# Opening the SBUF pools of a two-layer decoder trunk in another order

## The chip, the cores and the metric

The kernel runs on one core of a Trainium2 chip. The metric is device microseconds of one execution, median of the runs shown. The engines are TensorE (PE, with PEld for its weight loads), VectorE (DVE), ScalarE (ACT), GpSimd (POOL) and SyncE (SP), which issues nearly all DMAs.

## What is computed

Two decoder layers on 256 positions of 1024 channels, in float32. Each layer adds three normed branches to x:

```
for l in range(2):
    x = x + 0.5 * rms_norm(swiglu(rms_norm(x, g), w_gate, w_up, w_down), post_g)    # FFN 1
    x = x + rms_norm(hybrid_mix(rms_norm(x, g), w_in, ..., w_out), post_g)          # mixer
    x = x + 0.5 * rms_norm(swiglu(rms_norm(x, g), w_gate, w_up, w_down), post_g)    # FFN 2

def swiglu(h, w_gate, w_up, w_down):        # 1024 -> 2816 -> 1024
    return (silu(h @ w_gate) * (h @ w_up)) @ w_down
```

`hybrid_mix` projects the normed x to 2688 columns, runs four head groups over them (a gated convolution, a gated spatial mixing, an RWKV-7 recurrence in chunked form, a 31-tap convolution module), concatenates their 1024 channels and multiplies by `w_out`.

## The kernel before, in words

**Products.** Every large product is made from three float32r matmuls. A weight tile `raw` (128 x 1024 float32) is loaded by a DMA that SP issues, ACT rounds it to `whi`, DVE writes the rest `raw - whi` to `wlo` (`split`, lines 129 to 145). The left operand is split the same way into a high and a low part. `mm3` (lines 147 to 150) then adds three matmuls into one PSUM bank:

```
nc.tensor.matmul(dst, lhsT=sh, rhs=hi[:, c0:c0 + n], start=start, stop=False)   # L148
nc.tensor.matmul(dst, lhsT=sh, rhs=lo[:, c0:c0 + n], start=False, stop=False)   # L149
nc.tensor.matmul(dst, lhsT=sl, rhs=hi[:, c0:c0 + n], start=False, stop=stop)    # L150
```

`lhsT` is the stationary operand (128 x 128, loaded by a weight load of its own), `rhs` the moving one (mostly 128 x 512, that is 2048 contiguous bytes of each partition). Four kinds of product use it, and the profile names them by their PSUM tile:

- `pgu`: gate and up projection of an FFN. Stationary `xh`/`xl` (the normed x, pool `act`), moving `whi`/`wlo` (pool `wp`). 24 matmuls go to one bank before the next.
- `dn`: down projection of an FFN. Stationary `hh`/`hl` (made in `TR`, pool `work`, tag `c2`), moving `whi`/`wlo`. Each three matmuls change the bank, between two of the banks of tag `acc`.
- `pin`: input projections of the mixer. Stationary `xh`/`xl`, moving `whi`/`wlo`, 512, 384 or 256 columns.
- `wo`: output projection of the mixer. Stationary `yh`/`yl` (pool `wp`, tag `w2`), moving `whi`/`wlo`; like `dn` it changes between two banks each three matmuls, for block 1 in banks of the same tag `acc`.

Smaller float32 matmuls (transposes, the recurrence) fill the mixer's middle.

**Order of the work.** An FFN works on 11 slices of 256 hidden columns; for slice i it runs `pgu` for the position blocks 0 and 1 with the transposes of slice i-1 between them, and then `dn` of slice i-1 for both blocks. DMAs are issued by SP in program order, each when its `raw` buffer (4 of them) is free. The order of instructions on each engine is set by the framework's scheduler and by the places where the program pins an order.

**Pools.** A pool is a stretch of each SBUF partition. The pools lie one after another in the order in which they are opened (lines 52 to 56), and a tile takes the next multiple of 32 bytes:

```
const = ctx.enter_context(tc.tile_pool(name="const", bufs=1))
wp = ctx.enter_context(tc.tile_pool(name="wp", bufs=14))
rawp = ctx.enter_context(tc.tile_pool(name="rawp", bufs=4))
act = ctx.enter_context(tc.tile_pool(name="act", bufs=1))
work = ctx.enter_context(tc.tile_pool(name="work", bufs=2))
```

`const` ends at byte 20160 of the partition, in both kernels. The others hold, per partition:

| pool | what | bytes | bytes over a multiple of 64 |
|---|---|---|---|
| `wp` | 24 tiles of 4096 (`whi`, `wlo`, `yh`, `yl`, PB, PK, ...) | 98304 | 0 |
| `rawp` | 4 tiles `raw` of 4096 | 16384 | 0 |
| `act` | x, `xh`, `xl`, gp, ..., pc, zT, caT, zc | 54688 | 32 (caT takes 2080 bytes; of these tiles only zc lies behind it) |
| `work` | tags f2, f1, c2 (`hh`, `hl`), c1 and small ones | 37184 | 0 |

Within its pool every tile keeps its place. So the byte where a tile starts follows from where its pool starts. The tags f2, f1 and c2 of `work` start multiples of 64 bytes behind the pool's start.

Of the kernel before, what the change touches and what calls it, by code (L numbers as in the profile page):

```python
# [48 lines left out]
def trunk_kernel(ctx: ExitStack, tc: tile.TileContext, a, out):  # L49
    nc = tc.nc  # L50

    const = ctx.enter_context(tc.tile_pool(name="const", bufs=1))
    wp = ctx.enter_context(tc.tile_pool(name="wp", bufs=14))
    rawp = ctx.enter_context(tc.tile_pool(name="rawp", bufs=4))
    act = ctx.enter_context(tc.tile_pool(name="act", bufs=1))
    work = ctx.enter_context(tc.tile_pool(name="work", bufs=2))
    ps = ctx.enter_context(tc.tile_pool(name="ps", bufs=2, space=bass.MemoryType.PSUM))

    def acc_bank(name):
# [1069 lines left out]
```

## Time and profile before

| | us |
|---|---|
| median of 3 runs | 1041.27 (1040.5 to 1042.33) |
| the profiled execution | 1041.07 |
| its span, first to last instruction | 1039.3 |
| PE busy | 1015.2 (98%) |
| DVE, ACT, POOL busy | 668.1, 533.3, 69.5 |

The profile is of one execution. A matmul's end in it is modelled, so its duration (some 392 ns) overlaps the next one; what matmuls cost is read from their starts. The 1.8 us between the profiled execution's time and its span lie ahead of and behind the instructions.

### The profile page before, as it was taken

The page shows a single profiled execution, that of the slowest core. Times are in us where ns is not written, and L with a number is a line of the kernel's source. Part 1 is how long each engine was busy: PE and PEld are TensorE (multiplying, and loading weights), DVE is VectorE, ACT ScalarE, POOL GpSimd, SP SyncE. Part 2 cuts the span into 40 slices and gives each one's busy share as a digit, 9 for nine tenths or more (in the row PEclk, how much of TensorE's full clock was granted, in tenths as well). Part 3 has the DMA queues.
Part 4 walks back from the last instruction along what each step waited for, and adds up shares of the span by engine and source line. Part 5 has one row for each costly group of instructions (what it writes and reads, how often), then busy time and mean ns, then how long its engine had stood idle before and what let it go on. Part 6 is the DMA issues. An engine that isn't in the chain of part 4 may idle for free.

```text
span 1039.3 us, 13405 instructions
## 1 busy us (share of the span) xinstructions
PE 1015.2 (98%) x4898; PEld 832.2 (80%) x4898; DVE 668.1 (64%) x1044; ACT 533.3 (51%) x824; POOL 69.5 (7%) x133
## 2 busy tenths in 40 slices
PE   8999999999999999999999999999999999999997
PEld 6788888788797788888787888887878887888885
DVE  5765453689988755545575555447999885545533
ACT  7655353567466644535464435336655665444421
POOL 1000000210022100000010000013000130000000
PEclk9999999999999999999999999999999999999999
DMA  7985655344045756565556565635522367556521
GB/s 277 303 289 166 210 166 186 106 152 160 24 145 180 243 172 213 162 207 169 170 195 205 167 208 164 210 111 167 167 85 81 122 199 227 202 164 209 165 71 40
DMA packets 51474, 178.28 MB, mean 172 GB/s; under 512 B 6097, under 2 KB 6609, under 8 KB 51409
## 3 DMA queue, kind: packets, MB, share of 16 engines
q1 hardware_dynamic: 51120, 176.91, 52.2%
q8 instruction: 38, 0.62, 0.2%
q10 hardware_dynamic: 288, 0.52, 0.1%
q14 instruction: 28, 0.22, 0.1%
HBM read 176.36 MB, written 1.05 MB: 171 GB/s over the span
## 4 chain that ended last, share of the span: by engine, by line
PE 83%; DVE 8%; DMA 4%; ACT 2%; POOL 1%; issue 1%; SPq 0%; DVEq 0%; POOLq 0%; ACTq 0%
PE pgu L149 13%; PE pgu L150 13%; PE pgu L148 13%; PE dn L149 8%; PE dn L148 8%; PE dn L150 8%; DMA raw<-in_ffn 4%; PE pin L149 3%; PE pin L148 3%; PE pin L150 3%; PE hTp L348 2%; DVE wlo L141 1%; PE zp L676 1%; PE wo L148 1%; PE xT L178 1%
## 5 line engine op out<-in xcount | busy, mean ns | idle before, releaser
L141 DVE TENSOR_TENSOR wlo<-raw,whi 128x1024 fp32r<-128x1024 f32 (+1 forms) x320 | 388.8, 1219 | 161.8 <-ACT whi L140 146.3
L140 ACT CAST whi<-raw 128x1024 fp32r<-128x1024 f32 (+1 forms) x320 | 334.1, 1047 | 204.2 <-PE dn L149 107.6
L148 PE MATMUL pgu<-whi,xh 128*128 128x512 f32 x704 | 279.2, 397 | 2.7 <-ACT xh L237 2.2
L149 PE MATMUL pgu<-wlo,xh 128*128 128x512 f32 x704 | 275.6, 392 | 1.4 <-DVE wlo L141 1.4
L150 PE MATMUL pgu<-whi,xl 128*128 128x512 f32 x704 | 275.2, 391 | 0.0
L148 PEld LDWEIGHTS pgu<-whi,xh 128*128 128x128 f32 x704 | 132.6, 188 | 30.9 <-ACT xh L237 2.4
L149 PEld LDWEIGHTS pgu<-wlo,xh 128*128 128x128 f32 x704 | 132.5, 188 | 28.8 <-DVE wlo L141 2.1
L150 PEld LDWEIGHTS pgu<-whi,xl 128*128 128x128 f32 x704 | 132.4, 188 | 28.5
L148 PE MATMUL dn<-whi,hh 128*128 128x512 f32 x352 | 140.1, 398 | 3.8 <-ACT hh L352 3.8
L337 DVE SCALAR_TENSOR_TENSOR h<-pgu,rpre,silu 128x256 f32<-128x256 f32 x88 | 42.4, 482 | 153.1 <-ACT silu L335 152.9
L149 PE MATMUL dn<-wlo,hh 128*128 128x512 f32 x352 | 140.1, 398 | 0.0
L335 ACT ACTIVATE silu<-pgu,rpre 128x256 f32<-128x256 f32 x88 | 41.6, 472 | 188.7 <-PE pgu L150 187.4
L150 PE MATMUL dn<-whi,hl 128*128 128x512 f32 x352 | 136.8, 392 | 0.0
L148 PEld LDWEIGHTS dn<-whi,hh 128*128 128x128 f32 x352 | 66.2, 188 | 21.0 <-ACT hh L352 5.1
L150 PEld LDWEIGHTS dn<-whi,hl 128*128 128x128 f32 x352 | 65.8, 188 | 16.6 <-DVE hl L353 1.2
L149 PEld LDWEIGHTS dn<-wlo,hh 128*128 128x128 f32 x352 | 66.1, 188 | 14.7
L149 PE MATMUL pin<-wlo,xh 128*128 128x512 f32 (+2 forms) x192 | 70.8, 371 | 0.0
L148 PE MATMUL pin<-whi,xh 128*128 128x512 f32 (+2 forms) x192 | 70.5, 371 | 0.0
L150 PE MATMUL pin<-whi,xl 128*128 128x512 f32 (+2 forms) x192 | 70.5, 371 | 0.0
L835 DVE SCALAR_TENSOR_TENSOR zc<-zT,par,zc 128x256 f32<-128x256 f32 x120 | 49.8, 477 | 3.2 <-ACT zc L832 3.2
L149 PEld LDWEIGHTS pin<-wlo,xh 128*128 128x128 f32 x192 | 36.0, 188 | 5.4 <-DVE wlo L141 0.7
L150 PEld LDWEIGHTS pin<-whi,xl 128*128 128x128 f32 x192 | 36.3, 189 | 5.1 <-DVE xl L190 0.6
(216 smaller groups left out, 892.2 us busy)
## 6 DMA issues: line engine op xcount, KB each, us to landing
raw<-in_ffn SPq DMA_DIRECT2D x260, 512.0 KB, 4.5
raw<-in_wout SPq DMA_DIRECT2D x16, 512.0 KB, 4.4
raw<-in_win_z SPq DMA_DIRECT2D x8, 512.0 KB, 4.1
raw<-in_win_rk SPq DMA_DIRECT2D x8, 512.0 KB, 4.6
raw<-in_win_ca SPq DMA_DIRECT2D x8, 512.0 KB, 4.1
raw<-in_win_uv SPq DMA_DIRECT2D x8, 512.0 KB, 4.4
gp<-in_post_g SPq DMA_DIRECT2D x6, 512.0 KB, 4.8
raw<-in_win_vl SPq DMA_DIRECT2D x8, 384.0 KB, 3.2
```

The costliest lines, as they stand in the source:

```text
L140: i0 = nc.scalar.copy(hi[:, 0:n], raw[:, 0:n])
L141: i1 = nc.vector.tensor_tensor(out=lo[:, 0:n], in0=raw[:, 0:n], in1=hi.bitcast(F32)[:, 0:n], op=ALU.subtract)
L148: nc.tensor.matmul(dst, lhsT=sh, rhs=hi[:, c0:c0 + n], start=start, stop=False)
L149: nc.tensor.matmul(dst, lhsT=sh, rhs=lo[:, c0:c0 + n], start=False, stop=False)
L150: nc.tensor.matmul(dst, lhsT=sl, rhs=hi[:, c0:c0 + n], start=False, stop=stop)
L178: t = nc.tensor.transpose(tp[:, k * P:(k + 1) * P], x[b][:, kk * P:(kk + 1) * P], ident)
L335: nc.scalar.activation(out=s, in_=pg[:, 0:256], func=AF.Silu, scale=r)
L337: nc.vector.scalar_tensor_tensor(out=h, in0=pg[:, 256:512], scalar=r, in1=s, op0=ALU.mult, op1=ALU.mult)
L348: nc.tensor.transpose(tp[:, q * P:(q + 1) * P], h[:, j * P:(j + 1) * P], ident)
L676: nc.tensor.matmul(zp[:, h * P:(h + 1) * P], lhsT=PB[b][:, h, 1, :], rhs=S["Xm"][:, h, :], start=True, stop=True)
L835: nc.vector.scalar_tensor_tensor(out=zc[:, j, :], in0=zT[:, j, k:k + 256], scalar=w, in1=zc[:, j, :], op0=ALU.mult, op1=ALU.add)
```

## The change

After `const` the pools are opened in the order `work`, `act`, `wp`, `rawp`. Nothing else in the program is edited.

```
     const = ctx.enter_context(tc.tile_pool(name="const", bufs=1))
+    work = ctx.enter_context(tc.tile_pool(name="work", bufs=2))
+    act = ctx.enter_context(tc.tile_pool(name="act", bufs=1))
     wp = ctx.enter_context(tc.tile_pool(name="wp", bufs=14))
     rawp = ctx.enter_context(tc.tile_pool(name="rawp", bufs=4))
-    act = ctx.enter_context(tc.tile_pool(name="act", bufs=1))
-    work = ctx.enter_context(tc.tile_pool(name="work", bufs=2))
```

By the sizes above the pools start at these bytes:

| pool | before | over a multiple of 64 | after | over a multiple of 64 |
|---|---|---|---|---|
| `wp` | 20160 | 0 | 112032 | 32 |
| `rawp` | 118464 | 0 | 210336 | 32 |
| `act` | 134848 | 0 | 57344 | 0 |
| `work` | 189536 | 32 | 20160 | 0 |

## Rows read from the trace of the kernel before

**Rows 1.** The page: busy time, and the chain that ended last.
```profile
PE 1015.2 (98%) x4898; PEld 832.2 (80%) x4898; DVE 668.1 (64%) x1044; ACT 533.3 (51%) x824; POOL 69.5 (7%) x133
PE 83%; DVE 8%; DMA 4%; ACT 2%; POOL 1%; issue 1%; SPq 0%; DVEq 0%; POOLq 0%; ACTq 0%
```

**Rows 2.** Stages: time from:to, then busy us of PE, PEld, DVE, ACT, POOL; clock; DMA.
```profile
36.00:190.00 154.00, 154.00 (x690) 125.61 (x689) 86.51 (x88) 72.90 (x85) 3.11 (x4) 1.00 0.62 203
200.00:330.00 130.00, 125.66 (x741) 105.49 (x740) 117.77 (x283) 80.83 (x160) 17.21 (x35) 1.00 0.41 131
```

**Rows 3.** Groups by line and shape, one of each kind of three-matmul product.
```profile
L148 PE MATMUL pgu<-whi,xh 128*128 128x512 f32 x704 | 279.2, 397 | 2.7 <-ACT xh L237 2.2 <-ACT whi L140 0.4 <-ACT whi L279 0.2
L149 PE MATMUL dn<-wlo,hh 128*128 128x512 f32 x352 | 140.1, 398 | 0.0
L148 PE MATMUL pin<-whi,xh 128*128 128x512 f32 x128 | 51.0, 398 | 0.0
L149 PE MATMUL wo<-wlo,yh 128*128 128x512 f32 x64 | 26.1, 408 | 0.0
L148 PE MATMUL pin<-whi,xh 128*128 128x384 f32 x32 | 11.0, 344 | 0.0
L148 PE MATMUL pin<-whi,xh 128*128 128x256 f32 x32 | 9.2, 287 | 0.0
```

**Rows 4.** Timeline of PE, start first: pgu alone, ends of a run of 70.
```profile
337.98 0.39 PE L150 MATMUL pgu<-whi,xl 128*128 128x512 f32 x1
...
353.62 0.39 PE L150 MATMUL pgu<-whi,xl 128*128 128x512 f32 x1
```

**Rows 5.** Timeline of PE: a run of 24 dn and the pgu behind it.
```profile
101.97 0.39 PE L148 MATMUL dn<-whi,hh 128*128 128x512 f32 x1
102.20 0.40 PE L149 MATMUL dn<-wlo,hh 128*128 128x512 f32 x1
102.44 0.39 PE L150 MATMUL dn<-whi,hl 128*128 128x512 f32 x1
102.67 0.39 PE L148 MATMUL dn<-whi,hh 128*128 128x512 f32 x1
...
107.57 0.40 PE L148 MATMUL pgu<-whi,xh 128*128 128x512 f32 x1
```

**Rows 6.** Timeline of PE: wo of block 0, ends of a run of 14.
```profile
323.06 0.39 PE L148 MATMUL wo<-whi,yh 128*128 128x512 f32 x1
...
326.01 0.39 PE L149 MATMUL wo<-wlo,yh 128*128 128x512 f32 x1
```

**Rows 7.** Groups by line and shape: equal DVE and ACT operations on differently placed operands.
```profile
L190 DVE TENSOR_TENSOR xl<-xg,xh 128x512 fp32r<-128x512 f32 x20 | 13.2, 689 | 0.5 <-ACT xh L189 0.4
L189 ACT CAST xh<-xg 128x512 fp32r<-128x512 f32 x20 | 11.9, 617 | 5.5 <-DVE xg L182 5.4
L281 DVE TENSOR_TENSOR wlo<-raw,whi 128x512 fp32r<-128x512 f32 x8 | 5.3, 689 | 5.7 <-ACT whi L279 5.7
L279 ACT CAST whi<-raw 128x512 fp32r<-128x512 f32 x8 | 4.7, 616 | 3.9 <-DMA raw<-in_ffn 3.9
```

**Rows 8.** DMA issues: KB each, median us from issue to landing.
```profile
raw<-in_ffn SPq DMA_DIRECT2D x8, 256.0 KB, 5.4
xt<-in_xT SPq DMA_DIRECT2D x4, 256.0 KB, 5.5
```

**Rows 9.** The chain in order of time, mixer of layer 0: float32 matmuls of 128 columns.
```profile
280.04 1.79 PE zp L676 x16
...
284.32 0.89 PE wps L691 x8
```

**Rows 10.** Waits of PE itself: us in total, times, longest.
```profile
PE dn L148 <- ACT hh L352: 3.8, 3, 1.9
...
PE pgu L149 <- DVE wlo L141: 1.4, 2, 0.8
...
PE pgu L148 <- ACT whi L140: 0.4, 1, 0.4
```

## The prediction, made before the changed kernel was run

> **What bounds the kernel now.** The page first: PE is busy for 98% of the span and holds 83% of the chain that ended last, while DVE and ACT are busy for two thirds and half [rows 1]. [...] So the time is the sum of the distances from one matmul's start to the next. No instruction, wait or DMA is edited; the change can act only through what an operand's place in the partition does to the speed of an instruction. The question is which instructions care.
>
> The groups give the counts: three lines each of 704 `pgu`, 352 `dn`, 192 `pin` (128 + 32 + 32) and 64 `wo` [rows 3], that is 2112, 1056, 576 and 192 matmuls. Their listed means overlap (ends are modelled), so I read starts. An undisturbed run of `pgu` goes from 337.98 to 353.62 us in 69 steps, 226.7 ns each [rows 4]. A run of `dn` goes from 101.97 to 107.57 in 24 steps, 233.3 ns each, and evenly so: each three take 0.70 us [rows 5]. That is 6.7 ns more for the same 512 columns from the same weight pool. `wo` takes 226.9 (2.95 us in 13 steps) [rows 6]. `wo` is built as `dn` is (three matmuls to a bank, then the other bank) and reads the same moving tiles; block 1 of it writes the same kind of banks. What sets `dn` apart from both is where its stationary operand lies: `hh` and `hl` start 32 bytes over a multiple of 64, `xh`, `xl`, `yh`, `yl` and all moving tiles on one. I take that as the cause, short of proof: no other float32r matmul here has an operand off 64.
>
> **The change part by part.** There is one edit with these consequences: weights and raw tiles go from 64-byte starts to 32 over, the work pool from 32 over onto 64, the activations stay on 64 (only zc stays off it).
>
> *DVE and ACT: nothing.* The 128x512 subtraction takes 689 ns with `xg` (work pool, 32 over) and 689 with all operands on 64; the 128x512 cast takes 617 against 616 [rows 7]. If a nanosecond were there, it would lie behind PE.
>
> *DMA: nothing.* 256 KB loads into `xt` (32 over) land after 5.5 us, into `raw` (on 64) after 5.4, in the same stretch of the start [rows 8]. The difference is within their queueing; were it 0.1 us a load, the buffers ahead would cover it except at the FFN starts.
>
> *float32 matmuls: nothing.* `zp` reads both operands on 64: 1.79 us for 16 records, 112 ns. `wps` has its moving operand `zz` 32 over: 0.89 us for 8, 111 ns [rows 9].
>
> *float32r matmuls.* The stationary part has a price: 6.7 ns. The part that matters most, a moving operand 32 over, has no row: all 3936 read theirs on 64 before. [...] A gain from it I exclude by nothing but find no reason for. I take 6.7 ns: it is the nearest row, of the same instruction form and the same offset, and a stream of 2048 bytes meets the same boundaries as a load of 512. Then:
>
> - `pgu`: 2112 x 6.67 ns = +14.1 us (stationary on 64 as before, moving now off).
> - `pin`: 576 x 6.67 = +3.8 (the step taken as the same for 256 and 384 columns).
> - `dn`: the stationary comes onto 64 (-7.0), the moving goes off it (+7.0): 0.
> - `wo`: both operands go off. Two prices would be +2.6; if what counts is that the two differ, 0. I take one, +1.3.
>
> Sum +19.2 us. From it goes what is hidden: at the start of three FFNs and at the first slices of the kernel PE waits for weights that come by DMA, 3.8 + 1.4 + 0.4 us in all [rows 10]. The 70 `pgu` ahead of such a wait grow by 0.47 us each time, and the wait shrinks by that: some -1.4 over three. Elsewhere nothing hides a longer matmul, since PE is the chain. Net +17.8 on the profiled execution's 1041.07, which is 0.2 below the median of the runs: **1059**. The likeliest case's own range: without `wo` and with all 5.6 us of waits shrinking 14.1 + 3.8 - 5.6 = +12.3, with `wo` at 2.6 and nothing hidden +20.5: 1053 to 1062.
>
> **The rivals.**
>
> *Only the stationary operand's place counts (faster).* The price of `dn` is paid during the weight load's overlap with the stream, and the stream itself would run at its rate wherever it starts. Then `dn` gains 1056 x 6.67 = 7.0 us and `wo`, whose `yh`/`yl` move with `wp`, loses 1.3: -5.7, and another -1.5 or so if the uneven first steps of `pgu` behind each `dn` run go too; 1034 to 1036. For it: the float32 rows, where a moving operand off 64 is free [rows 9]. It decides where the moving price is under 5.7 / 3936 = 1.5 ns. The same sign comes if not the 64 bytes but the high end of the partition is what slows `hh`/`hl`, for `work` moves to the low end; then the last of the weight slots would pay instead.
>
> *The place counts for nothing (no change).* Then `dn` has its 233.3 ns for another reason, such as a state of PE's queues that its waits set up, and the time stays at 1041. For it: DVE, ACT, DMA and float32 matmuls all ignore the offset [rows 7 to 9]. Against it: `wo` with the same structure settles at 226.9 [rows 6]. [...] That the schedule itself could change with the addresses, so that more than addresses differ, I count here with a small part: the scheduler works with buffers of tags, which are the same.
>
> *The moving operand costs more than 6.7 ns*, say twice: +38 us, 1079. Nothing in the trace asks for it.
>
> **How the numbers follow.** Forecast (both operands count, or their difference does) 0.47; stationary alone or high end 0.30; no effect 0.19; twice the price 0.04. About 0.2% (2.1 us) is what a measurement of this kernel can tell from no change. Slower gets 0.47 + 0.04 = 0.51, less a little for a moving price so small that `dn`'s gain cancels it: 0.50. Faster 0.30. Same 0.20. Cases of both signs hold most of the chance, so the range reaches from the stationary-only case to the upper end of the forecast: 1034 to 1063, beside 1053 to 1062 for the likeliest alone.
>
> **What would show it.** If the forecast is right, runs of `pgu` show steps of 233 ns instead of 226.7 and `dn` stays at 233; PE stays at 98%; DVE, ACT and DMA rows keep their durations. If the stationary alone counts, `pgu` stays at 226.7 and `dn` comes down to 227. `wo` tells one price (233) from two (240) or none (227). If `dn` keeps 233 and `pgu` 227, the place isn't the cause. I am wrong in the mechanism if DVE or ACT durations move, or if the order of instructions differs.

## The result, and the profile after

The changed kernel takes **1053.48 us** (median of 4 runs, 1052.45 to 1054.64), beside 1041.8 for the kernel before on the same chip (4 runs, 1040.5 to 1044.8): a ratio of **1.0108 [1.0083, 1.0134]**, slower by 11.7 us. The profiled execution took 1052.45 us, with a span of 1050.7, 11.4 more than before. One run among all those below, of the last experiment, took 1725.28 us at a granted clock of 0.616, and its median and ratio leave it out.

The page of the changed kernel, busy time and the chain that ended last, to read against [rows 1]:

```profile
PE 1028.6 (98%) x4898; PEld 835.0 (79%) x4898; DVE 667.7 (64%) x1044; ACT 533.0 (51%) x824; POOL 69.5 (7%) x133
PE 85%; DVE 7%; DMA 3%; ACT 2%; POOL 1%; issue 1%; SPq 0%; DVEq 0%; POOLq 0%; ACTq 0%
```

Same counts, and each engine has its instructions in the same order as before. PE alone is busier, by 13.4 us. DVE, ACT and POOL are not. The granted clock of the two stages of [rows 2] is 1.00 again. The groups by line and shape, the same four as in [rows 7]:

```profile
L190 DVE TENSOR_TENSOR xl<-xg,xh 128x512 fp32r<-128x512 f32 x20 | 13.1, 686 | 0.5 <-ACT xh L189 0.4
L189 ACT CAST xh<-xg 128x512 fp32r<-128x512 f32 x20 | 11.9, 616 | 5.6 <-DVE xg L182 5.5
L281 DVE TENSOR_TENSOR wlo<-raw,whi 128x512 fp32r<-128x512 f32 x8 | 5.3, 688 | 5.7 <-ACT whi L279 5.7
L279 ACT CAST whi<-raw 128x512 fp32r<-128x512 f32 x8 | 4.6, 612 | 3.9 <-DMA raw<-in_ffn 3.9
```

Here the placings have swapped (`xg` is on 64 now, `raw`, `whi` and `wlo` are 32 over) and the durations stay within 4 ns: 686 and 688 ns on DVE, 616 and 612 on ACT. The DMA issues of the start, as [rows 8] (KB each, median us to landing), and PE's longest wait for ACT, as the first of [rows 10]:

```profile
raw<-in_ffn SPq DMA_DIRECT2D x8, 256.0 KB, 5.6
xt<-in_xT SPq DMA_DIRECT2D x4, 256.0 KB, 5.1
```

```profile
PE dn L148 <- ACT hh L352: 2.8, 3, 1.1
```

`raw` went from 5.4 to 5.6 and `xt` from 5.5 to 5.1. In the runs below the medians go from 5.0 to 5.8 for `raw` and from 4.8 to 6.1 for `xt`, with no order by place, so no effect of the place shows. The wait at the FFN starts fell from 3.8 to 2.8 us. So the time lies in the distances between matmul starts. The timeline of PE, start first: a run of 24 `dn` with the `pgu` behind it, 14 `wo`, and a run of 70 `pgu`, as [rows 4 to 6]:

```profile
103.33 0.39 PE L148 MATMUL dn<-whi,hh 128*128 128x512 f32 x1
...
108.92 0.40 PE L148 MATMUL pgu<-whi,xh 128*128 128x512 f32 x1
...
326.02 0.39 PE L148 MATMUL wo<-whi,yh 128*128 128x512 f32 x1
...
328.96 0.39 PE L149 MATMUL wo<-wlo,yh 128*128 128x512 f32 x1
...
341.07 0.40 PE L150 MATMUL pgu<-whi,xl 128*128 128x512 f32 x1
...
357.24 0.40 PE L150 MATMUL pgu<-whi,xl 128*128 128x512 f32 x1
```

`pgu` takes 16.17 us for 69 steps, 234.3 ns each instead of 226.7. `dn` stays at 233 (5.59 us in 24). `wo` stays at 226 (2.94 us in 13), though now both its operands lie 32 over a multiple of 64. The table sums all start-to-start distances of the two profiled executions, each counted for the matmul that begins it. The last column is what the distances above 260 ns (waits and hand-overs) hold beyond a step of 227 ns each, a step being the distance from one start to the next:

| product | before, us | after, us | difference | of it, shorter stalls |
|---|---|---|---|---|
| `pgu`, 2112 | 494.2 | 506.0 | +11.8 | -0.6 |
| `pin`, 576 | 127.1 | 127.7 | +0.6 | -0.6 |
| `dn`, 1056 | 247.3 | 247.2 | -0.1 | 0.0 |
| `wo`, 192 | 50.9 | 50.9 | 0.0 | -0.1 |
| all other matmuls | | | -1.0 | |
| sum | | | +11.4 | |

Practically all of it is `pgu`. The question left is why `pgu` pays, `dn` stays and `wo` does not pay. Below, the settled step of a run of matmuls is the mean step once its pattern repeats.

### The profile page after: what moved, and what is told of

Read it like the earlier page. It is cut to its first block, busy times and chain, and to the rows that moved or that the text cites. A ratio compares the mean times of both kernels' runs of the same rounds, so it can differ in the third digit from the quotient of the medians.

```text
span 1050.7 us, 13405 instructions
## 1 busy us (share of the span) xinstructions
PE 1028.6 (98%) x4898; PEld 835.0 (79%) x4898; DVE 667.7 (64%) x1044; ACT 533.0 (51%) x824; POOL 69.5 (7%) x133
## 4 chain that ended last, share of the span: by engine, by line
PE 85%; DVE 7%; DMA 3%; ACT 2%; POOL 1%; issue 1%; SPq 0%; DVEq 0%; POOLq 0%; ACTq 0%
PE pgu L149 14%; PE pgu L148 14%; PE pgu L150 14%; PE dn L148 8%; PE dn L150 8%; PE dn L149 8%; PE pin L149 3%; DMA raw<-in_ffn 3%; PE pin L148 3%; PE pin L150 3%; PE hTp L348 2%; PE zp L676 1%; PE wo L148 1%; PE wo L149 1%; PE xT L178 1%
## 5 line engine op out<-in xcount | busy, mean ns | idle before, releaser
L148 PE MATMUL pgu<-whi,xh 128*128 128x512 f32 x704 | 283.5, 403 | 1.9 <-ACT xh L237 1.5
L149 PE MATMUL pgu<-wlo,xh 128*128 128x512 f32 x704 | 280.3, 398 | 1.6 <-DVE wlo L141 1.4
L150 PE MATMUL pgu<-whi,xl 128*128 128x512 f32 x704 | 279.3, 397 | 0.0
L148 PEld LDWEIGHTS pin<-whi,xh 128*128 128x128 f32 x192 | 36.3, 189 | 5.4 <-ACT whi L140 0.4
```

## The experiments

All of them pad tiles by some bytes, which moves what lies behind; no instruction changes its form or its place in its engine's order. Ratios are against the kernel before, run on the same chip. Where a sum of distances is given it is of the profiled execution.

### Does each operand's own place modulo 64 count?

**Work pool onto 64, everything else as before.** The pool order of before, zc padded by 32 bytes at the end of `act`:

```
-        zc = act.tile([P, 2, 256], F32, name="zc")
+        zc = act.tile([P, 520], F32, name="zc")[:, 0:512].rearrange("p (j t) -> p j t", j=2)
```

> Pools in the order of before, with 32 bytes more at the end of act, so that hh/hl come onto a multiple of 64 and every operand of the three-matmul products lies on one; hh/hl stay at the high end of the partition. Difference theory (a step is 226.7 ns once settled where both operands start at the same place within 64 bytes, 233 to 234 otherwise): dn falls from 233.4 to about 227, 1056 x 6.4 = -6.8 us, and the uneven first steps of pgu behind each dn settle sooner, -1.5: ratio to before 0.992. Theory that each operand off 64 costs on its own: the same. Theory that only the moving operand counts and dn has a reason of its own: dn stays at 233, ratio 1.000. Theory that the high end of the partition slows hh/hl: also 1.000.

Measured: 1036.97 us, ratio 0.9953 [0.9935, 0.9971]. Faster, but by less than expected: `dn` lost 4.0 us, not 6.8. Its run in the timeline, 24 steps:

```profile
102.06 0.39 PE L148 MATMUL dn<-whi,hh 128*128 128x512 f32 x1
...
107.56 0.39 PE L148 MATMUL pgu<-whi,xh 128*128 128x512 f32 x1
```

5.50 us in 24 steps is 229 ns, in an even pattern of 229, 232, 226. With every operand of `dn` on 64 the step should have been 227. So 64 bytes is not the whole of it: there are more than two levels. The high end of the partition isn't the reason either, since `hh` and `hl` still lie there.

**Everything 32 bytes over.** A constant padded, so that every pool behind it moves; distances between tiles stay:

```
-    dpar = const.tile([P, L, 8], F32, name="dpar")
+    dpar = const.tile([P, L, 12], F32, name="dpar")
```

> Pools in the order of before, with 32 bytes more in const: all other pools move by 32. Weights, raw, activations lie 32 over a multiple of 64, hh/hl on one. Difference theory: pgu, pin and wo have both operands off alike and stay at 227, dn still differs and stays at 233: ratio 1.000 (within 0.002). Each operand off 64 costs: pgu has two prices, at least +11.8 us as the moving one alone gave in the changed kernel, ratio 1.012 or more. Only the moving one counts: 1.011.

Measured: 1042.38 us, ratio 1.0002 [0.9989, 1.0016]. The timeline, a run of 24 `dn` and 69 steps of `pgu`:

```profile
103.83 0.39 PE L148 MATMUL dn<-whi,hh 128*128 128x512 f32 x1
...
109.43 0.40 PE L148 MATMUL pgu<-whi,xh 128*128 128x512 f32 x1
...
339.93 0.39 PE L150 MATMUL pgu<-whi,xl 128*128 128x512 f32 x1
...
355.58 0.39 PE L150 MATMUL pgu<-whi,xl 128*128 128x512 f32 x1
```

`pgu` at 15.65 / 69 = 226.8 ns with both operands 32 over a multiple of 64, and `dn` at 5.60 / 24 = 233.3 with the stationary now on 64 and the moving operand over. Nothing changed where only absolute places did. So the reading that each operand pays for its own place modulo 64 fails.

### Is it the difference of the two places?

**Moving operand alone over.** The same constant and the x of block 0 padded by 32 bytes each, so that `xh` and `xl` come back onto a multiple of 64; `wp` is moved by 32 bytes, `hh` by 64 and so stays 32 over:

```
-    x = [act.tile([P, D], F32, name=f"x{b}") for b in range(NB)]
+    x = [act.tile([P, D + 8 * (b == 0)], F32, name=f"x{b}")[:, 0:D] for b in range(NB)]
-    dpar = const.tile([P, L, 8], F32, name="dpar")
+    dpar = const.tile([P, L, 12], F32, name="dpar")
```

> Pools in the order of before, with 32 bytes more in const and 32 more ahead of x1: weights and raw 32 over a multiple of 64, xh/xl on one, hh/hl 32 over as before. So pgu and pin differ, dn and wo have both operands off alike. Difference theory: pgu 234 (+11.8 us), pin +0.6, dn 227 (-6.8), wo unchanged: +5.6 us, ratio 1.005. Only the moving one counts: pgu +11.8, dn at 233 or more: 1.011. Each operand off 64 costs: dn pays twice, about 240, +11.8 + 7: 1.018.

Measured: 1047.5 us, ratio 1.0045 [1.0031, 1.0059]. The same stretches:

```profile
102.24 0.40 PE L148 MATMUL dn<-whi,hh 128*128 128x512 f32 x1
...
107.75 0.40 PE L148 MATMUL pgu<-whi,xh 128*128 128x512 f32 x1
...
339.21 0.40 PE L150 MATMUL pgu<-whi,xl 128*128 128x512 f32 x1
...
355.31 0.39 PE L150 MATMUL pgu<-whi,xl 128*128 128x512 f32 x1
```

`pgu` rises to 16.10 / 69 = 233.3 ns (+9.1 us in all), `dn` falls to 5.51 / 24 = 229.6 (-3.7 us). The ratio is the 1.005 expected by the difference modulo 64, but its parts are not: +11.8 and -6.8 were expected, and `dn` at 227.

**New pool order, both operands on 64.** The changed kernel with the 32-byte pad of zc, which puts `wp` on a multiple of 64 again:

> Pools in the order of the change, with 32 bytes more at the end of act: wp and rawp come onto a multiple of 64, so every operand of the three-matmul products lies on one. Difference theory, and the theory that each operand off 64 costs: pgu 227, dn 227: ratio to before 0.992, the same as the old order with all on 64; the order of the pools is then worth nothing by itself. If the order or the far end of the partition costs something of its own, it stays above 1.000. If the granule is 128 or 256 bytes (xh/xl and whi/wlo start 64 apart here), pgu stays at 234.

Measured: 1046.75 us, ratio 1.0039 [1.0022, 1.0055]: a miss for the difference modulo 64, which expected 0.992. Of what was expected, only the last alternative, a granule of 128 or 256 bytes, has `pgu` stay dear.

```profile
102.72 0.40 PE L148 MATMUL dn<-whi,hh 128*128 128x512 f32 x1
...
108.19 0.40 PE L148 MATMUL pgu<-whi,xh 128*128 128x512 f32 x1
...
339.63 0.39 PE L150 MATMUL pgu<-whi,xl 128*128 128x512 f32 x1
...
355.74 0.39 PE L150 MATMUL pgu<-whi,xl 128*128 128x512 f32 x1
```

`pgu` stays at 16.11 / 69 = 233.5 ns (+10.6 us) with both operands on 64, and `dn`, also with both on 64, settles at 227 after seven uneven steps (-5.0 us). If it is the difference of the two starts that counts, its period must be longer than 64 bytes: here `pgu` has a distance of 64 bytes modulo 256, and `dn` of 0.

Ordered by that distance (start of the stationary tile less start of the moving one, modulo 256), the runs so far agree with each other. Distances 0, 32, 160 and 192 each occur at two pairs of places, and each has one step to within 0.3 ns, so it is the distance that counts and not the places:

| kernel, product | stationary, moving, modulo 256 | distance | settled step, ns |
|---|---|---|---|
| before, `pgu` | 192, 192 | 0 | 226.7 |
| everything 32 over, `pgu` | 224, 224 | 0 | 226.8 |
| new order on 64, `dn` | 192, 192 | 0 | 226.7 |
| after, `dn` | 192, 160 | 32 | 233 |
| moving alone over, `pgu` | 0, 224 | 32 | 233.3 |
| new order on 64, `pgu` | 0, 192 | 64 | 233.5 |
| after, `pgu` | 0, 160 | 96 | 234.3 |
| before, `dn` | 96, 192 | 160 | 233.3 |
| everything 32 over, `dn` | 128, 224 | 160 | 233.3 |
| work pool on 64, `dn` | 128, 192 | 192 | 229 |
| moving alone over, `dn` | 160, 224 | 192 | 229 |

### How long is the period?

**Work pool 256 bytes apart, and 0 apart, modulo 512.** The pool order of before, zc with 96 bytes of padding (first kernel) and with 352 (second); the edit is that of the first experiment with 536 and 600 for 520:

> Pools in the order of before, 96 bytes more at the end of act: hh/hl start 256 bytes apart from whi/wlo when both starts are taken modulo 512 (modulo 256 they agree). The runs so far say that the step depends on the distance of the two starts, and on more of it than the last 64 bytes. If the period is 256 bytes: dn settles at 226.7 ns as wo does, 1056 x 6.7 = -7.0 us, and pgu behind it settles sooner, -1.5: ratio 0.992. If it is 512 bytes or more: dn stays between 229 and 234, ratio 0.995 to 1.000.

> Pools in the order of before, 352 bytes more at the end of act: hh/hl start at the same place as whi/wlo and xh/xl modulo 512, so all products but the short float32 ones have distance 0. Distance theory, whatever its period up to 512: dn settles at 226.7 ns, ratio 0.992, about 1033 us. If dn had a reason of its own beside the distance, it stays above 229 as with 192 bytes distance: 0.995.

Measured: 1034.52 us, ratio 0.9930 [0.9910, 0.9951], and 1034.7 us, ratio 0.9928 [0.9909, 0.9947]. They agree within their intervals, so the period is 256 and not 512. The timeline, 24 `dn` of the first and of the second:

```profile
101.45 0.39 PE L148 MATMUL dn<-whi,hh 128*128 128x512 f32 x1
...
106.89 0.39 PE L148 MATMUL pgu<-whi,xh 128*128 128x512 f32 x1
...
103.70 0.39 PE L148 MATMUL dn<-whi,hh 128*128 128x512 f32 x1
...
109.14 0.39 PE L148 MATMUL pgu<-whi,xh 128*128 128x512 f32 x1
```

5.44 us in 24 steps in both, 226.7 ns, without uneven steps at the start. In the first kernel `dn` fell by 6.0 us and `pgu` by 2.0. Of the latter, 1.4 are the uneven first steps behind each `dn` run, which are gone too.

**A sweep of the distance.** The kernel of 0 apart, with `hh` and `hl` of each FFN slice starting a given number of bytes into larger tiles (o counts floats):

```
+            o = OFF[2 * l + f][i] // 4
+            hh = work.tile([P, 5 * P], F32R, name="hh", tag="c2", bufs=C2)
+            hl = work.tile([P, 5 * P], F32R, name="hl", tag="c2", bufs=C2)
+            hh, hl = [t[:, o:o + 4 * P].rearrange("p (q t) -> p q t", q=4) for t in (hh, hl)]
```

> As the kernel with distance 0, but hh/hl of each FFN slice lie a stated number of bytes further in a longer tile: 0 to 96 in FFN 1 of layer 0, 112 to 240 in FFN 2, 256 to 384 and 400 to 508 in layer 1, mostly in steps of 16. pgu keeps distance 0 throughout. Distance theory: the settled step of dn follows the distance, 226.7 ns at 0, 233.4 at 32, 233.3 at 64, 234 at 96, 233.3 at 160, 229.2 at 192; what lies between and whether 256 is as good as 0 is open. If 64-byte multiples alone counted, every multiple of 64 would give 226.7; the kernel with 64 bytes between xh and whi already speaks against that.

Measured, the mean of 18 of the 24 steps of the `dn` run at each distance (without the first five and the last), one run each; 112, 248 and 252 are read at 368, 504 and 508:

| distance | ns | distance | ns | distance | ns |
|---|---|---|---|---|---|
| 0 | 226.7 | 80 | 231.9 | 192 | 228.9 |
| 8 | 230.8 | 96 | 234.1 | 208 | 231.9 |
| 16 | 226.7 | 112 | 233.3 | 224 | 233.2 |
| 32 | 233.3 | 128 | 232.7 | 240 | 226.7 |
| 48 | 233.3 | 144 | 226.7 | 248 | 233.3 |
| 64 | 233.3 | 160 | 233.3 | 252 | 226.7 |
| | | 176 | 230.3 | | |

Distances above 256 repeat those below to 0.1 ns: 272 gives 226.7 as 16, 336 gives 231.9 as 80, 352 gives 234.1 as 96, 432 gives 230.3 as 176, 448 gives 228.9 as 192. Set aside are the runs at the starts of three FFNs, behind a wait: the one at 256 needed 16 uneven steps before it settled at 226.7, and the one at 400 didn't settle in its 24 and averaged 233.3, where its partner 144 takes 226.7. The timeline at 16, 32, 160 and 288 (32 again):

```profile
86.15 0.39 PE L154 MATMUL dn<-whi,hh 128*128 128x512 f32 x1
...
91.59 0.39 PE L154 MATMUL pgu<-whi,xh 128*128 128x512 f32 x1
...
102.97 0.39 PE L154 MATMUL dn<-whi,hh 128*128 128x512 f32 x1
...
108.56 0.39 PE L154 MATMUL pgu<-whi,xh 128*128 128x512 f32 x1
...
407.68 0.39 PE L154 MATMUL dn<-whi,hh 128*128 128x512 f32 x1
...
413.28 0.40 PE L154 MATMUL pgu<-whi,xh 128*128 128x512 f32 x1
...
579.36 0.39 PE L154 MATMUL dn<-whi,hh 128*128 128x512 f32 x1
...
584.95 0.39 PE L154 MATMUL pgu<-whi,xh 128*128 128x512 f32 x1
```

5.44, 5.59, 5.60 and 5.59 us for 24 steps. This is within one kernel and one execution, and by the edit only the start of `hh` and `hl` differs from slice to slice. The sweep took 1040.56 us in a single run, since most of its slices lie at a dear distance.

### Does the new order cost anything of itself?

**New pool order, all distances 0.** The changed kernel with the x of block 0 padded by 448 bytes and zc by 96, so that `whi` and `wlo`, `xh` and `xl`, `hh` and `hl` all start at the same place modulo 512:

```
-    x = [act.tile([P, D], F32, name=f"x{b}") for b in range(NB)]
+    x = [act.tile([P, D + 112 * (b == 0)], F32, name=f"x{b}")[:, 0:D] for b in range(NB)]
-        zc = act.tile([P, 2, 256], F32, name="zc")
+        zc = act.tile([P, 536], F32, name="zc")[:, 0:512].rearrange("p (j t) -> p j t", j=2)
```

> Pools in the order of the change, with 448 bytes more ahead of x1 and 96 more at the end of act, so that xh/xl, hh/hl, yh/yl and whi/wlo all start at the same place modulo 512. Distance theory: pgu and dn settle at 226.7 ns, ratio 0.992 to before, the same as the old order with distance 0; so the order of the pools costs nothing by itself. If weights at the far end or activations at the near end cost something: above 0.995.

Measured: 1035.34 us (median of five runs), ratio 0.9940 [0.992, 0.996].

```profile
104.40 0.39 PE L148 MATMUL dn<-whi,hh 128*128 128x512 f32 x1
...
109.84 0.39 PE L148 MATMUL pgu<-whi,xh 128*128 128x512 f32 x1
...
339.33 0.39 PE L150 MATMUL pgu<-whi,xl 128*128 128x512 f32 x1
...
354.97 0.39 PE L150 MATMUL pgu<-whi,xl 128*128 128x512 f32 x1
```

`dn` takes 5.44 / 24 = 226.7 ns and `pgu` 15.64 / 69 = 226.7: the longer steps of the changed kernel are gone. With the same pool order, 544 bytes of padding take 18 us from the changed kernel's 1053.48, and the interval overlaps that of the old order at distance 0. So no cost of the order shows beyond the distances that it makes; one under the width of the intervals, some 0.4%, is not excluded. The fastest versions are those of the old order with 96 or 352 bytes of padding, 0.993 of before.

## Why the prediction was right and wrong

**The bound, and what doesn't care.** Right. Only the steps of float32r matmuls changed; DVE, ACT and DMA kept their times, and the other matmuls moved by -1.0 us in sum, about as far as in the other runs (-0.7 to +1.8). The float32 `zp` and `wps` keep their steps of 112 and 111 ns (1.79 us for 16 and 0.89 for 8, as in [rows 9]).

**The cause of `dn`'s 233 ns: this step failed.** The prediction put it on the stationary operand's own place ("What sets `dn` apart from both is where its stationary operand lies"). What counts is how far the stationary start lies from the moving one, modulo 256 bytes. Moving everything by 32 bytes changed nothing, and with every operand of `dn` on 64 it took 229, not 227. The difference was in the prediction, but only as one of two readings for `wo`, and modulo 64; the rows of before hold three products at distances 0, 160 and 0, which can't tell the two apart. Reading places modulo 64 was a choice that no row supported.

**`pgu`, +14.1 forecast, +11.8 measured.** The step reached 234, close to the 233.4 forecast, though not because the moving operand was off 64: in the new order with both on 64 it still pays 6.7 ns. The size fell short since before not all steps stood at 226.7. Behind each `dn` run come some eight uneven ones (behind the run of [rows 5]: 233, 236, 224, 231, 236, 228, 233, 231, and then 227), and behind most transposes three, so the mean was 227.7; and some 150 of the 2112 distances are stalls or hand-overs, which don't pay. That leaves 1960 x 6.4 ns = 12.6, less 0.6 of shorter stalls and 0.2 in the hand-overs to `dn`.

**`pin`, +3.8 forecast, +0.6 measured: mis-sized.** Only the 384 matmuls of 512 columns pay, and they stood at 229.7 ns already in their short runs between other work. The step rose to 234.1, and with the waits among them, which shrank, 84.4 us became 85.7. Those of 384 and 256 columns went from 16.6 to 16.4 and from 11.1 to 11.1 us: no price shows for narrower streams at this distance. Taking the same step for all widths was wrong.

**`dn`, 0 forecast, -0.1 measured.** Right by accident. No gain of 7.0 met a loss of 7.0: its distance went from 160 to 32, and both cost 233.3.

**`wo`, +1.3 forecast, 0.0 measured.** Its two operands lie in one pool and move together, which was the lower end given ("if what counts is that the two differ, 0").

**Hidden, -1.4 forecast, -1.0 measured, not shown.** The wait at the three FFN starts went from 3.8 to 2.8 us. It is `dn` waiting for `hh`, which ACT makes behind a cast of weights that waited for its DMA (the first of the three in the trace before, a cast at 354.3 us), as the prediction took it. But in the runs whose `pgu` stands at 226.7 the same wait is anything from 2.7 to 5.2 us, so this fall can't be put down to the longer `pgu`. Distances above 260 ns shrank by 1.3 us in the four products, but 0.6 of that is in `pin`, where nothing was forecast.

**The rivals.** With the stationary alone counting, `dn` should have come down to 227 and `pgu` stayed; instead `dn` stayed and `pgu` rose. The high end of the partition falls with the faster kernels in the old order, whose `hh` and `hl` stay there. That places count for nothing falls with the result and with the faster kernels. Twice the price falls with the step of `pgu`, 7.6 ns above the cheap one. The forecast, slower by both or by their difference, was right in sign; the measured 1053.48 lies at the low end of its own range, 1053 to 1062, and +11.7 us is two thirds of the +17.8 forecast.

**How much of it was luck.** The sign, in part. Read by 64, the new order with all operands on 64 should have been faster, 0.992; it was slower, 1.0039. That the change itself came out slower rests on a distance of 96 for `pgu`, which the prediction didn't look at. The range over all cases, 1034 to 1063, takes in faster, same and slower, so that the result lies inside says little.

What stays open: what in the chip has the period of 256 bytes, and whether it is the weight load or the stream that is held up (the mean recorded duration of a load stays at 188 to 189 ns in the four products, before and after). All stationary tiles of a product start alike modulo 256, so these runs also can't tell whether the distance counts between the two operands of one matmul or between a stream and the load for the next one. Stationary operands of another width, or matmuls of another type, were not tried, nor `hh` moved without `hl`.

## What to carry to other kernels

Where TensorE is the bound and its 512-column float32r matmuls run back to back, start the stationary and the moving tiles at the same place modulo 256 bytes: 226.7 ns a step here, against up to 234.1 at other distances. In this kernel 96 bytes of padding are worth 0.7%, and a reordering of pools without it cost 1.1%. Read the spacing of starts of each kind of product in the timeline, and where two kinds of one shape differ, compare the two operands' addresses with each other, not each with a boundary. An edit that changes no instruction still changes addresses, so compare versions of a kernel only when these are held equal or known.

## What was not expected of the hardware

- The settled step of 512-column float32r matmuls, each with its own weight load, has many levels between 226.7 and 234.1 ns, not two, and they depend on the distance of the two starts modulo 256 bytes. They aren't smooth in it: 16 and 240 bytes cost nothing (226.7), 8 and 32 do (230.8 and 233.3).
- Steps at a dear distance repeat in a fixed pattern (229, 232, 226 at 192), and the same patterns come back at distances 256 apart.
- Behind a stall, transposes or a run at another distance, up to some ten steps of 224 to 240 ns (16 in one run of the sweep) pass before the even 226.7 at distance 0; behind the `dn` runs at 192 with the work pool on 64 there are none. At 144 the state in which a run begins seems to decide: 226.7 behind a `pgu` run, 233.3 behind a wait (at 400, the same place; one case each).
